# Rotating an 8192 x 8192 matrix: the first loads over four buffers, the last macro tile in two halves with four output buffers

## The chip, the cores and the metric

The kernel runs on one core of a Trainium2 chip. The metric is the device time of one execution in microseconds (us).

PE is the matmul engine, DVE the vector engine, ACT the scalar engine, SP the engine whose queue issues the loads. "DMA engines" are the 16 engines that move data between the memory (HBM) and the core's own memory. One DMA instruction is split over all 16.

## The reference

```python
def reference(x, k):          # x: 8192 x 8192 float32, k = 1
    return np.rot90(x, k)
```

So out[8191 - c, r] = x[r, c]: a transpose with the rows of the result in reverse order. No arithmetic: 268.4 MB are read and 268.4 MB are written.

## The kernel before

The matrix is cut into 16 macro tiles of 1024 rows and 4096 columns. The last of them is cut further, into pieces of 2048, 1024 and 1024 columns. A macro tile has eight loads of 2 MB; each load is reversed in blocks by eight copies on DVE, into 68 small buffers. When all rows of the macro tile are there, PE transposes 4 blocks of 128 columns at a time for all 1024 rows, ACT copies the result out of PE's accumulation memory in two halves, and one store of 2 MB goes out ("an output"). Loads and outputs are numbered 0 to 127 here.

```python
def macro_tiles(N, M):
    for r0 in range(0, N, R):                 # R = 1024
        widths = [W] * (M // W)               # W = 4096
        ...
        if r0 + R == N:
            widths[-1:] = [2048, 1024, 1024]
        ...
    a_pool = ... bufs=2     # load buffers, 2 MB each
    r_pool = ... bufs=68    # reversed chunks, a macro tile needs 64
    o_pool = ... bufs=2     # output buffers, 2 MB each
    for r0, c0, C in tiles:
        last = (r0, c0, C) == tiles[-1]
        q = W // C
        for t0 in range(0, RT, q):
            if loads < 2:
                a = o_pool.tile([P, W], dt, tag="o")
            else:
                a = a_pool.tile([P, W], dt, tag="a")
            loads += 1
            nc.sync.dma_start(out=a, in_=x[...])             # load, issued by SP
            ... 8 x nc.vector.tensor_copy(...[:, :, ::-1])   # reversal on DVE
        for g0 in range(0, C // P, G):                       # G = 4
            ot = o_pool.tile([P, W], dt, tag="o")
            S = PW if last and g0 + G == C // P else G       # PW = 2
            for h in range(0, G, PW):
                ... 16 x nc.tensor.transpose(ps..., chunks..., ident)
                nc.scalar.copy(o[...], ps[:])                # 1.87 us
                done = h + PW
                if done % S == 0:
                    nc.scalar.dma_start(out=dst, in_=o[...]) # store, issued by ACT
```

A load buffer is free again when its eight reversals are done. An output buffer is free when its store has landed.

Of the kernel before, what the change touches and what calls it, by code (L numbers as in the profile page):

```python
# [2 lines left out]

# [5 lines left out]

P = 128  # L10




R = 1024
RT = R // P
W = 4096
CH = 512
G = 4
PW = 2  # L20


def whole_reads(nc):






    for fn in nc.m.functions:  # L30
        for block in fn.blocks:
            for n, ins in enumerate(block.instructions):
                if not isinstance(ins, mybir.InstDMACopy):
                    continue
                src = ins.ins[0]
                ap = [list(d) for d in src.ap]
                if len(ap) == 3 and ap[2][0] == 1 and ap[1][0] == ap[2][1]:
                    ap = [ap[0], [1, 1], [1, ap[1][1] * ap[2][1]]]
                    block.instructions[n] = copy.replace(
                        ins,  # L40
                        ins=[copy.replace(src, ap=ap)],
                        ant_dge_precooked=False,
                    )


def macro_tiles(N, M):

    for r0 in range(0, N, R):
        widths = [W] * (M // W)
        if r0 == 0:  # L50
            widths[:1] = [4096]
        if r0 + R == N:
            widths[-1:] = [2048, 1024, 1024]
        c0 = 0
        for C in widths:
            yield r0, c0, C
            c0 += C


@with_exitstack  # L60
def kernel(
    ctx: ExitStack,
    tc: tile.TileContext,
    x: bass.AP,
    k: bass.AP,
    out: bass.AP,
):
    nc = tc.nc
    assert k == 1, f"only k=1 supported, got {k}"
    nc.at_finalize(whole_reads)  # L70

    N, M = x.shape
    dt = x.dtype

    consts = ctx.enter_context(tc.tile_pool(name="consts", bufs=1))
    ident = consts.tile([P, P], dt)
    make_identity(nc, ident)

    a_pool = ctx.enter_context(tc.tile_pool(name="a_pool", bufs=2))
    r_pool = ctx.enter_context(tc.tile_pool(name="r_pool", bufs=68))  # L80
    o_pool = ctx.enter_context(tc.tile_pool(name="o_pool", bufs=2))
    psum_pool = ctx.enter_context(
        tc.tile_pool(name="psum", bufs=2, space=bass.MemoryType.PSUM)
    )

    tiles = list(macro_tiles(N, M))
    loads = 0
# [3 lines that stand above are left out]
        chunks = {}  # L91
        for t0 in range(0, RT, q):

            if loads < 2:
                a = o_pool.tile([P, W], dt, tag="o")
            else:
                a = a_pool.tile([P, W], dt, tag="a")
            loads += 1
            a = a.rearrange("r (q c) -> r q c", q=q)
            nc.sync.dma_start(  # L100
                out=a,
                in_=x[r0 + t0 * P : r0 + (t0 + q) * P, c0 : c0 + C].rearrange(
                    "(q r) c -> r q c", q=q
                ),
            )


            for u in range(q):
                for j in range(C // CH):
                    ar = r_pool.tile([P, CH // P, P], dt, tag="ar")  # L110
                    nc.vector.tensor_copy(  # L111
                        out=ar[:],
                        in_=a[:, u, j * CH : (j + 1) * CH].rearrange(
                            "r (b m) -> r b m", m=P
                        )[:, :, ::-1],
                    )
                    chunks[t0 + u, j] = ar

        for g0 in range(0, C // P, G):
            ot = o_pool.tile([P, W], dt, tag="o")  # L120
            o = ot.rearrange("m (g f) -> m g f", g=G)
            S = PW if last and g0 + G == C // P else G
            for h in range(0, G, PW):
                ps = psum_pool.tile([P, PW, R], mybir.dt.float32)
                for w in range(PW):
                    g = g0 + h + w
                    for t in range(RT):
                        nc.tensor.transpose(  # L128
                            ps[:, PW - 1 - w, t * P : (t + 1) * P],
                            chunks[t, g * P // CH][:, g % (CH // P), :],  # L130
                            ident,
                        )
                nc.scalar.copy(o[:, G - PW - h : G - h, :], ps[:])  # L133

                done = h + PW
                if done % S == 0:
                    top = M - c0 - (g0 + done) * P
                    dst = out[top : top + S * P, r0 : r0 + R].rearrange(
                        "(g m) f -> m g f", g=S
                    )  # L140
                    nc.scalar.dma_start(  # L141
                        out=dst, in_=o[:, G - done : G - done + S, :]
                    )


# [1 line left out]
_INS = ['x', 'k']  # L147
_OUTS = [((8192, 8192), 'float32')]

_NUMBERS = {'k': 1}  # L150


# [26 lines left out]
```

## Time and profile before

| | before |
|---|---|
| time, median of the first 3 runs | 1275.13 us |
| bytes moved | 537.55 MB |
| rate in the middle | about 428 GB/s |
| bytes at that rate, worked out (537.55 / 0.428) | 1256 us |

The page's first part has the span and the busy time of each engine with its share of the span.

```profile
span 1274.2 us, 10388 instructions
...
PE 719.2 (56%) x4096; PEld 685.5 (54%) x4096; DVE 355.2 (28%) x1024; ACT 466.9 (37%) x257; POOL 0.7 (0%) x6
```

No engine that computes is near its limit. The page's second part cuts the span in 40 slices of 31.9 us; the lines below are the busy share of the DMA engines in tenths, and what they moved.

```profile
DMA  9999999999999999999999999999999999999998
GB/s 375 366 427 427 427 428 431 429 428 428 430 428 430 428 427 429 429 429 429 427 427 427 429 427 428 427 427 429 428 427 426 424 423 429 427 425 422 420 408 338
```

The rate stands at 427 to 431 GB/s in most of the span and is low in the first two slices and the last two. What can be gained without moving fewer bytes lies there.

The timeline shows the start. Each line has start, duration, engine, source line and operation, the number of merged instructions, and in brackets how long the engine stood idle before and what ended that. The lines are the reversals of loads 3 to 7, and the issue of the first store.

```profile
22.76 2.77 DVE L111 COPY ar<-a 128x512 f32<-128x512 f32 x8 [2.12 <-DMA a<-in_x_dram]
...
29.79 2.77 DVE L111 COPY ar<-a 128x512 f32<-128x512 f32 x8 [4.25 <-DMA a<-in_x_dram]
...
35.39 2.77 DVE L111 COPY ar<-a 128x512 f32<-128x512 f32 x8 [2.83 <-DMA a<-in_x_dram]
...
42.46 2.77 DVE L111 COPY ar<-a 128x512 f32<-128x512 f32 x8 [4.29 <-DMA a<-in_x_dram]
...
47.89 2.77 DVE L111 COPY ar<-a 128x512 f32<-128x512 f32 x8 [2.66 <-DMA a<-in_x_dram]
...
54.41 0.64 ACTq L141 DMA_DIRECT2D out_dram<-ot  x1
```

The first four loads come 4.9 us apart, which is full rate for 2 MB. Then the steps are 7.0, 5.6, 7.1 and 5.4 us: only two load buffers are left in rotation, and a load can be issued only when the reversals of the load two before are done.

The end, in windows of 5 us. The columns are the window, its length, the busy time of PE, PE's weight loads, DVE, ACT and POOL with the number of instructions, the granted clock, the busy share of the DMA engines and, last, GB/s.

```profile
1240.00:1245.00 5.00, 3.74 (x32) 3.46 (x32) 0.00 (x0) 2.08 (x2) 0.00 (x0) 1.00 0.91 386
1245.00:1250.00 5.00, 1.76 (x9) 1.76 (x10) 2.77 (x8) 3.64 (x2) 0.00 (x0) 0.83 0.68 288
1250.00:1255.00 5.00, 4.79 (x36) 4.55 (x35) 0.00 (x0) 3.09 (x2) 0.00 (x0) 0.83 0.85 357
1255.00:1260.00 5.00, 3.26 (x30) 2.98 (x29) 0.00 (x0) 3.15 (x3) 0.00 (x0) 1.00 0.90 374
1260.00:1265.00 5.00, 3.05 (x28) 2.77 (x26) 0.00 (x0) 2.49 (x2) 0.00 (x0) 1.00 0.88 374
1265.00:1270.00 5.00, 0.00 (x0) 0.00 (x0) 0.00 (x0) 2.17 (x2) 0.00 (x0) 0.54 0.95 393
1270.00:1275.00 5.00, 0.00 (x0) 0.00 (x0) 0.00 (x0) 0.00 (x0) 0.00 (x0) 0.50 0.45 187
```

From 1245 us on the rate stays at 187 to 393 GB/s: the last outputs share two buffers, each waits for a store to land and then for two copies of ACT.

### The profile page before, as it was taken

How to read it: one execution, taken by the hardware profiler on the slowest of the kernel's cores; microseconds unless marked ns; L12 is line 12 of the kernel's file. 1: busy time of each engine (PE TensorE's matmuls, PEld its weight loads, DVE VectorE, ACT ScalarE, POOL GpSimd, SP SyncE). 2: the span in 40 equal slices, each digit the busy share in tenths (PEclk: the TensorE clock that was granted, in tenths of full speed). 3: DMA queues.
4: the chain of work that ended last, by engine and by line, in shares of the span. 5: the costliest groups of instructions: out<-in, count | busy, mean ns of one | idle time of the engine just before them, and what ended most of it. 6: DMA issues, size and time to landing. Idle time of an engine off the chain costs nothing.

```text
span 1274.2 us, 10388 instructions
## 1 busy us (share of the span) xinstructions
PE 719.2 (56%) x4096; PEld 685.5 (54%) x4096; DVE 355.2 (28%) x1024; ACT 466.9 (37%) x257; POOL 0.7 (0%) x6
## 2 busy tenths in 40 slices
PE   1455556556655665556546565565565665665564
PEld 0355556555554655556546555565555554665564
DVE  4422232223222322232223222322232222321210
ACT  0233343334334333343334333433343333434444
POOL 0000000000000000000000000000000000000000
PEclk9968686877777677776886867768777778678878
DMA  9999999999999999999999999999999999999998
GB/s 375 366 427 427 427 428 431 429 428 428 430 428 430 428 427 429 429 429 429 427 427 427 429 427 428 427 427 429 428 427 426 424 423 429 427 425 422 420 408 338
DMA packets 39105, 537.55 MB, mean 422 GB/s; under 512 B 4112, under 2 KB 4112, under 8 KB 6160
## 3 DMA queue, kind: packets, MB, share of 16 engines
q1 hardware_dynamic: 20480, 268.44, 49.8%
q10 hardware_dynamic: 18576, 268.44, 49.8%
q8 instruction: 32, 0.52, 0.2%
q14 instruction: 17, 0.14, 0.0%
HBM read 268.44 MB, written 268.44 MB: 421 GB/s over the span
## 4 chain that ended last, share of the span: by engine, by line
DMA 84%; DVE 12%; issue 2%; ACT 1%; PE 0%; DVEq 0%; SPq 0%; ACTq 0%
DMA a<-in_x_dram 81%; DVE ar L111 12%; DMA out_dram<-ot 3%; ACT ot L133 1%; PE ps L128 0%; DVEq L111 0%; SPq L100 0%; ACTq L133 0%; ACTq L141 0%
## 5 line engine op out<-in xcount | busy, mean ns | idle before, releaser
L128 PE MATMUL ps<-ident,ar 128*128 128x128 f32 x4096 | 719.2, 358 | 543.8 <-ACT ot L133 500.2
L128 PEld LDWEIGHTS ps<-ident,ar 128*128 128x128 f32 x4096 | 685.5, 192 | 577.3 <-ACT ot L133 530.5
L133 ACT COPY ot<-ps 128x2048 f32<-128x2048 f32 x256 | 465.6, 1870 | 789.3 <-DMA out_dram<-ot 733.5
L111 DVE COPY ar<-a 128x512 f32<-128x512 f32 x1024 | 355.2, 421 | 894.4 <-DMA a<-in_x_dram 894.4
L133 ACT ACT_TABLE_LOAD x1 | 1.3, 1283 | 10.9 <-DVE ar L111 10.9
masks.py:199 POOL TENSOR_SCALAR_AFFINE_SELECT ident<-ident 128x128 f32<-128x128 f32 x1 | 0.3, 292 | 0.1
masks.py:197 POOL MEMSET ident<- 128x128 f32 x1 | 0.2, 204 | 0.3 <-POOLq L160 0.3
L160 POOL MEMSET const-bfloat16-1.0<- 128x1 bf16 x1 | 0.1, 102 | 0.0
L160 POOL MEMSET const-uint8-127<- 128x1 uint8 x1 | 0.1, 102 | 0.0
L160 POOL MEMSET const-float32-0.0<- 128x1 f32 x1 | 0.1, 99 | 0.2 <-issue 0.2
L160 POOL MEMSET const-float32-1.0<- 128x1 f32 x1 | 0.1, 99 | 0.0
## 6 DMA issues: line engine op xcount, KB each, us to landing
a<-in_x_dram SPq DMA_DIRECT2D x128, 2048.0 KB, 16.6
out_dram<-ot ACTq DMA_DIRECT2D x127, 2048.0 KB, 15.9
out_dram<-ot ACTq DMA_DIRECT2D x2, 1024.0 KB, 5.7
```

Of the source, the lines that this page charges most:

```text
L111: nc.vector.tensor_copy(out=ar[:], in_=a[:, u, j * CH : (j + 1) * CH].rearrange("r (b m) -> r b m", m=P)[:, :, ::-1],)
L128: nc.tensor.transpose(ps[:, PW - 1 - w, t * P : (t + 1) * P], chunks[t, g * P // CH][:, g % (CH // P), :], ident,)
L133: nc.scalar.copy(o[:, G - PW - h : G - h, :], ps[:])
L160: nc = _bacc.Bacc("TRN2", target_bir_lowering=False, num_devices=1)
```

## The change

Its intent is to fill both ends. The first eight loads rotate over the two load and the two output buffers (the latter are not needed before the first output), so that loads 4 to 7 need not wait. The last macro tile is cut in two halves of 2048 columns, and the four outputs of the last half alternate between load and output buffers, since no load needs them any more.

```diff
--- before.py
+++ after.py
@@ -14,6 +14,7 @@
 
 R = 1024
 RT = R // P
+LAST = [2048, 2048]
 W = 4096
 CH = 512
 G = 4
@@ -47,10 +48,8 @@
 
     for r0 in range(0, N, R):
         widths = [W] * (M // W)
-        if r0 == 0:
-            widths[:1] = [4096]
         if r0 + R == N:
-            widths[-1:] = [2048, 1024, 1024]
+            widths[-1:] = LAST
         c0 = 0
         for C in widths:
             yield r0, c0, C
@@ -91,7 +90,8 @@
         chunks = {}
         for t0 in range(0, RT, q):
 
-            if loads < 2:
+
+            if loads < RT and loads % 4 >= 2:
                 a = o_pool.tile([P, W], dt, tag="o")
             else:
                 a = a_pool.tile([P, W], dt, tag="a")
@@ -117,7 +117,11 @@
                     chunks[t0 + u, j] = ar
 
         for g0 in range(0, C // P, G):
-            ot = o_pool.tile([P, W], dt, tag="o")
+
+            if last and g0 // G % 2 == 0:
+                ot = a_pool.tile([P, W], dt, tag="a")
+            else:
+                ot = o_pool.tile([P, W], dt, tag="o")
             o = ot.rearrange("m (g f) -> m g f", g=G)
             S = PW if last and g0 + G == C // P else G
             for h in range(0, G, PW):
```

The order of the transposes on PE and of the copies on ACT does not change. The last four loads have half-size (2048 columns) instead of quarter-size rows, so DVE reverses the last 32 chunks in another order.

## The prediction

> **What bounds it.** The DMA. The chain that ended last is 84% DMA; PE is busy 56%, ACT 37%, DVE 28%. The forty slices show 427 to 431 GB/s nearly throughout; only the ends are lower: 375 and 366 in the first two, 408 and 338 in the last two. The Trainium skill ("DMA: Bandwidth & Descriptors", Specifications) gives 435 GB/s as fabric ceiling; the trace's plateau of 428 agrees. 537 MB at 428 GB/s is an estimated 1256 us of the 1274 us span. So some 18 us are lost, at the two ends, part of it unavoidable (first and last latency). The change moves no fewer bytes, so it cannot gain 2% (25 us).
>
> **Start.** The timeline shows reversals starting, as loads land, at 8.1, 13.0, 17.9, 22.8 us (4.9 apart, full rate), then 29.8, 35.4, 42.5, 47.9: loads 4 to 7 rotate over two buffers, and each waits for the reversal (2.77 us) of the load two before. The first load takes 7.4 us from issue to landing, so about 2.5 us of latency lies bare every second load. The last four take 25.1 us instead of 19.6. With four buffers load 7 should land at about 42.4, the first output be issued near 49 instead of 54.4. Windows of 5 us from 0 to 65 lack 8.6 us of transfer against 428 GB/s; 2.3 of it is the first latency, about 0.9 stays. Gain about 5.4 us, all on the critical path: the steady state is bound by bytes and merely shifts.
>
> **End.** Windows of 5 us from 1200 lack about 8.7 us, 2.0 of it the last latency; the worst are 288 GB/s (1245 to 1250), then 357, 374, 374, 393: the last outputs have two buffers, and each waits for a store, then 3.64 us of ACT copies, then the latency. The change gives the last four outputs four buffers, so they run back to back. Against it: all four need the last load. From its landing I count about 7 us to the next output's issue (reversal, transposes, two copies of 1.87 us) plus 2 us to its first bytes, covered only by earlier outputs, still on two buffers. The skill (same page, Queues, rings and completion order) says a DMA engine alternates between rows packet by packet; this fits the trace: with loads of 2048 columns (half-size packets) loads take about 13 us and outputs 7.9, instead of 9.8 each. Replaying the measured durations by hand I estimate the last load landing near 1242 (old clock), two gaps of about 1.5 us, and a gain of about 2.5 us.
>
> **Nothing else moves:** the order of instructions on PE, DVE, ACT is the same; only the last four loads change shape.
>
> **Prediction: 1267 us**, 80% range 1261.5 to 1272. Chances: faster by over 2% 0.01, within 2% 0.98, slower 0.01.
>
> **Right if:** reversals start every 4.9 us through the eighth; the second slice rises from 366 to above 410 GB/s; DVE work is 5 to 6 us earlier from then on; the middle stays at 427 to 431; the last three outputs' ACT copies wait for no store, and the final 20 us run near 428, with one or two short gaps around the last load's landing.
>
> **Wrong if:** the first outputs come too late to fill the time after load 9, giving the start's gain back; or the last load lands after the earlier outputs are gone, opening a gap of 5 us or more before the last four, so the end is even or worse; or the gaps near the end vanish altogether, giving 1262.

## More of the kernel before

The page's third and fourth parts give the DMA queues (packets, MB, share of 16 engines; q1 and q10 carry the kernel's loads and stores) and, last line, the chain of work that ended last, by engine.

```profile
q1 hardware_dynamic: 20480, 268.44, 49.8%
q10 hardware_dynamic: 18576, 268.44, 49.8%
q8 instruction: 32, 0.52, 0.2%
...
DMA 84%; DVE 12%; issue 2%; ACT 1%; PE 0%; DVEq 0%; SPq 0%; ACTq 0%
```

84% of the chain is DMA. The line q8 will matter later: it is not data of the kernel but instructions, 32 packets of 16 KB.

## The result, and the profile after

The changed kernel took 1271.54 us (median of 4 runs, 1271.33 to 1272.35) against 1274.65 us in the same job: ratio 0.9974, 95% interval 0.9951 to 0.9996. A ratio is the mean time of one kernel's fast runs over that of the other's fast runs of the same rounds, so it is not quite the ratio of the medians. Two later jobs gave 0.9963 and 0.9960. So the gain is 3.3 to 5.1 us; the prediction had 8.

The same lines of the page as before, after the change: span, GB/s of the 40 slices, the chain by engine.

```profile
span 1269.5 us, 10387 instructions
...
GB/s 400 416 430 428 429 427 430 430 428 429 428 429 429 428 429 429 428 430 429 429 428 427 423 428 428 429 428 429 425 423 429 428 421 424 424 427 418 421 385 357
...
DMA 79%; ACT 14%; DVE 4%; PE 1%; issue 1%; ACTq 0%; DVEq 0%
```

The second slice rose from 366 to 416 GB/s. The last two, 408 and 338 before, are 385 and 357. The chain is still DMA for the most part, but now 14% of it, some 174 us, is ACT. That is not the end: four outputs are only 15 us of copies. In the middle of the span the chain now runs through outputs (54% of it are stores), with a copy of 3.64 us between one store and the next; before it ran through loads (81%) and their reversals on DVE (12%). The start, same lines of the timeline as before:

```profile
22.69 2.77 DVE L111 COPY ar<-a 128x512 f32<-128x512 f32 x8 [2.12 <-DMA a<-in_x_dram]
...
27.57 2.77 DVE L111 COPY ar<-a 128x512 f32<-128x512 f32 x8 [2.11 <-DMA a<-in_x_dram]
...
32.47 2.77 DVE L111 COPY ar<-a 128x512 f32<-128x512 f32 x8 [2.12 <-DMA a<-in_x_dram]
...
38.17 2.77 DVE L111 COPY ar<-a 128x512 f32<-128x512 f32 x8 [2.93 <-DMA a<-in_x_dram]
...
43.02 2.77 DVE L111 COPY ar<-a 128x512 f32<-128x512 f32 x8 [2.08 <-DMA a<-in_x_dram]
...
49.55 0.65 ACTq L145 DMA_DIRECT2D out_dram<-ot  x1
```

Five steps of 4.9 us, one of 5.7 (32.47 to 38.17), and then 4.9 again; the eighth reversal starts at 43.0 instead of 47.9 us and the first store is issued at 49.6 instead of 54.4. The end, in windows of 5 us, with cuts:

```profile
1195.00:1200.00 5.00, 1.80 (x17) 1.56 (x15) 0.32 (x1) 0.00 (x0) 0.00 (x0) 1.00 0.96 375
...
1205.00:1210.00 5.00, 4.35 (x25) 4.11 (x23) 2.05 (x7) 0.00 (x0) 0.00 (x0) 0.68 1.02 328
...
1230.00:1235.00 5.00, 2.94 (x14) 2.94 (x15) 0.00 (x0) 3.63 (x2) 0.00 (x0) 0.50 0.59 252
...
1240.00:1245.00 5.00, 4.41 (x41) 4.09 (x40) 0.00 (x0) 3.96 (x3) 0.00 (x0) 1.00 0.75 318
1245.00:1250.00 5.00, 4.42 (x41) 4.15 (x40) 0.00 (x0) 4.00 (x3) 0.00 (x0) 1.00 0.99 419
...
1255.00:1260.00 5.00, 0.29 (x3) 0.05 (x1) 0.00 (x0) 2.58 (x2) 0.00 (x0) 0.94 1.00 419
...
1265.00:1270.00 5.00, 0.00 (x0) 0.00 (x0) 0.00 (x0) 0.00 (x0) 0.00 (x0) 0.50 0.28 115
```

The low stretch from 1245 on is gone. In its place there are two windows with a gap (252 and 318 GB/s), two slow windows earlier (375 and 328), and the final drain stays at 413 to 419, with 115 in the last window. I counted what the windows lack of 428 GB/s, until the end of the span: 8.7 us from 1200 us on before, 9.0 us from 1195 us on after. **The loss at the end moved; it did not shrink.**

The waits of ACT in the last 30 us, before (first) and after (second): who it waited for, total us, times, longest.

```profile
ACT ot L133 <- DMA out_dram<-ot: 8.6, 3, 4.2
ACT ot L133 <- PE ps L128: 1.9, 1, 1.9
```

```profile
ACT ot L137 <- PE ps L132: 2.7, 4, 0.7
```

The waits for a store are gone, as intended. So what the change was made to remove was removed, and the time did not follow. That is what the experiments are about.

### The profile page after: what moved, and what is told of

It reads as the page before. It is cut to its first block, busy times and chain, and to the rows that moved or that the text cites. A ratio compares the mean times of both kernels' runs of the same rounds, so it can differ in the third digit from the quotient of the medians.

```text
span 1269.5 us, 10387 instructions
## 1 busy us (share of the span) xinstructions
PE 705.9 (56%) x4096; PEld 665.4 (52%) x4096; DVE 355.2 (28%) x1024; ACT 467.5 (37%) x257; POOL 0.7 (0%) x6
## 4 chain that ended last, share of the span: by engine, by line
DMA 79%; ACT 14%; DVE 4%; PE 1%; issue 1%; ACTq 0%; DVEq 0%
DMA out_dram<-ot 54%; DMA a<-in_x_dram 25%; ACT ot L137 14%; DVE ar L111 4%; PE ps L132 1%; ACTq L145 0%; ACTq L137 0%; DVEq L111 0%
## 5 line engine op out<-in xcount | busy, mean ns | idle before, releaser
L132 PE MATMUL ps<-ident,ar 128*128 128x128 f32 x4096 | 705.9, 352 | 549.4 <-ACT ot L137 469.4
L132 PEld LDWEIGHTS ps<-ident,ar 128*128 128x128 f32 x4096 | 665.4, 188 | 589.6 <-ACT ot L137 501.0
```

The source lines that it names most:

```text
L132: nc.tensor.transpose(ps[:, PW - 1 - w, t * P : (t + 1) * P], chunks[t, g * P // CH][:, g % (CH // P), :], ident,)
```

## The experiments

Where an experiment compares two kernels of one job, both were measured beside the kernel before, in the same five rounds on the same chip. An edit is shown against the changed kernel unless said otherwise.

### 1. The two parts by themselves

My theory was that the start delivers its gain and the end gives nothing.

**Start alone** (the end as before):

```diff
-LAST = [2048, 2048]
+LAST = [2048, 1024, 1024]
-            if last and g0 // G % 2 == 0:
+            if False:
```

> Only the first loads rotate over four buffers; the last macro tile is split 2048, 1024, 1024 as before. My theory (the start delivers, the end does not): the first eight loads land 4.9 us apart, the transferred bytes run 5.5 to 6 us ahead of the kernel before from 50 us on, and nearly all of it arrives at the end: 1268.5 to 1270 us, ratio about 0.9955. Rival (the start's gain is given back later, in the middle or at the old end): ratio 0.9975 to 1.0.

Measured: 1272.0 us against 1276.6 us, ratio 0.9969 (0.9957 to 0.9982), so 4.0 us (0.0031 x 1276). The loads do land 4.9 us apart and the transferred bytes are 5.9 us of transfer ahead of the kernel before at 100 us and 6.4 us ahead at 1140 us. But of these 6 us only 4 reach the end, by the ratio's interval between 2.3 and 5.5. That is between the two expectations, and it does not exclude the 5.4 us of the prediction.

**End alone** (the start as before):

```diff
-            if loads < RT and loads % 4 >= 2:
+            if loads < 2:
```

> Only the last macro tile is changed (two halves of 2048, the last four outputs over four buffers); the first loads as before. My theory: even or worse than before by up to 2 us (ratio 1.000 to 1.0015), with gaps of about 2 and 1.3 us in the DMA some 35 us before the end, where the outputs of the first half wait for one of two buffers. Rival (the end gains the 2.5 us predicted, the start is what fell short): ratio 0.998.

Measured: 1276.27 us, ratio 1.0006 (0.9993 to 1.0019). The end gains nothing; the predicted 2.5 us (0.998) is outside the interval.

**End alone, but all outputs on two buffers:**

```diff
-            if loads < RT and loads % 4 >= 2:
+            if loads < 2:
-            if last and g0 // G % 2 == 0:
+            if False:
```

> The last macro tile in two halves of 2048, but all outputs on two buffers; the first loads as before. If the four buffers do useful work in the changed kernel, this is slower than the run with them alone by 3 to 5 us (six outputs instead of two wait about 1 to 2 us each for a store, copies and the DMA's latency): ratio 1.002 to 1.004. If the buffers do not matter, equal to it.

Measured: 1276.29 us, ratio 1.0005 (0.9992 to 1.0017). A miss: the four buffers were to be worth 3 to 5 us over two, and are worth nothing that can be measured (by the means 0.2 us, the other way round, with two standard errors of 1.1). Experiment 4 looks for the reason.

**The whole change again:**

> The changed kernel itself, timed in five rounds beside its parts. Expected 1271 to 1272 us, ratio 0.9970 to 0.9978 as in the first result; if the parts add up, its difference from before is the sum of that of the start alone and of the end alone, within 1 us.

Measured: 1271.08 us, ratio 0.9963 (0.9951 to 0.9976), a little below the ratio expected. The parts add up: 4.0 us from the start, nothing from the end, 4.7 us for both, within the intervals.

These rounds hold a second reading of each part. "End alone" and the whole change differ only in the start: 1276.54 against 1271.10 us by the means, so 5.4 us (give or take 0.8; this and the like below are two standard errors, from the scatter of the runs). "Start alone" and the whole change differ only in the end: 1271.86 against 1271.10, so 0.8 us (give or take 0.7). In full length the start is thus worth 4.0 to 5.4 us, the end somewhere between nothing and 1 us.

### 2. Where does the start's gain go on the way?

A load or store counts as landed when the slowest of its 16 DMA engines is done. The trace has the 16 landings of every DMA. From them, the time between the first and the last engine of a DMA (median over the stretch):

```
stretch of the span      before     start alone
100 to 200 us            3.6 us     2.5 us
1000 to 1130 us          4.6 us     8.3 us
```

And the lead of the start alone over the kernel before, in one profile of each, at the same number of reversals and of issued stores:

```
number    reversal   store issue   mean
16        4.2 us     8.2 us        6.2 us
110       2.7 us     7.3 us        5.0 us
119       2.7 us     5.0 us        3.9 us
```

In this pair the bytes stay 6 us ahead, the finished DMAs do not. My reading: in the long middle the engines drift apart, the fast ones run ahead as far as the buffers let them, and the lead of the whole bytes is partly theirs. It is worth nothing at the end, since the slowest engine decides.

The other full-length profiles bear this out only in part. From 1000 to 1130 us the two others with the old start ("end alone" and the same on two buffers) have 5.7 and 6.6 us between first and last engine, the eight with the changed start 7.6 to 8.4. The lead of the changed kernel at the last landing of a load, from load 16 to load 110, falls from 6.0 to 4.1 us over "end alone", but over the run on two buffers it goes from 5.3 to 6.1 and does not fall. So how much of the lead is lost differs from profile to profile.

If the reading is right, the gain must depend on how long the middle is. The rival is that the old end meets the loads and stores in another phase and gives back the same amount whatever the length. I ran both kernels over the first and the last 1024 rows only, 4 macro tiles instead of 16 (the result is wrong: the other rows of x are not turned):

```diff
-    for r0 in range(0, N, R):
+    for r0 in (0, N - R):
```

> The kernel before, but only the first and the last 1024 rows of x are turned (4 macro tiles instead of 16; the result is wrong on purpose): the length over which the 16 DMA engines can drift apart is a quarter. Serves as the base of start_short. About 1275 minus three quarters of 1252 us (12 macro tiles of 78.2 us each at the pace of the middle), so 335 to 340 us.

> The start change alone, in the same shortened form (wrong on purpose). In the full length the start alone gained 4.0 us, though 5.8 us of bytes were ahead. My theory: the difference is lost because in the long middle the engines drift further apart (first to last engine of one DMA 8 us instead of 4.6), and with a quarter of the length they drift less: start_short is 5 to 6 us faster than before_short, and the spread of its landings before the end is under 4 us. Rival (what is given back is due to the form of the end, met in another phase, whatever the length): 4 us faster or less, as in full length.

Measured: 332.59 (335 to 340 were expected) and 324.89 us, so 7.7 us faster by the medians, with landings about 2.5 us apart in the middle of the short run with the changed start. A second job with the same two kernels:

> The kernel before, shortened, again as base of these rounds: 331 to 334 us; start_short_2 is 6 to 8 us faster than it, where the start alone gained 4 us in full length.

> The start change alone, shortened, again as base of these rounds: 324.5 to 325.5 us.

Measured: 333.19 and 325.76 us, 7.4 us. With the new end in both kernels (the two runs of experiment 3) it is 332.47 against 324.69 by the means, 7.8 us. So the start's gain is 7.4 to 7.8 us over a quarter of the length and 4.0 to 5.4 us over the whole. The rival has fallen as I had put it: the end is the same in both lengths, and does not give back the same amount. That the gain is smaller over the long middle is shown; that the drift of the engines makes it so is argued, since no run changes the drift alone. The gain in the short form is more than the 5 to 6 us I had expected and more than the lead of bytes (5.8 us); I have no full account of the excess. One part points the right way: in the short kernel before, the engines are 3.7 to 4.6 us apart, in the one with the changed start 2.5.

### 3. Is the new end worth more while the engines are close together?

The theory was that the end's 2.5 us are eaten by the same spread. Then they must show in the short form. The edits are those of experiment 2 on the changed kernel and on the end alone.

> The whole change in the shortened form (4 macro tiles, wrong on purpose). Compared with start_short_2 of the same rounds it shows what the new end is worth where the engines are little apart (spread of landings about 2.5 us instead of 8). Theory (the end's gain of 2.5 us is eaten by the engines being apart when the last tile begins): 1.5 to 3 us faster than start_short_2. Rival (the new end is worth nothing by its own form, whatever the spread): within 1 us of start_short_2.

> The end change alone in the shortened form (wrong on purpose), against before_short_2 of the same rounds. Theory: faster by 1 to 3 us. Rival: within 1 us of it, as in full length.

Measured: the whole change 324.75 us against 325.76 for the start alone; the end alone 332.93 us against 333.19. By the means, 0.9 us (give or take 0.8) and 0.5 us (give or take 1.6). The second pair decides little, but the first excludes the 2.5 us. The theory has fallen: the new end measures under 1 us by its own form, with the engines together or apart.

### 4. Why four buffers do not beat two at the end

This needs no new run. The ACT timeline of the last five outputs of "end alone" (four buffers): the issues of its stores.

```profile
1246.06 0.55 ACTq L145 DMA_DIRECT2D out_dram<-ot  x1
...
1250.38 0.55 ACTq L145 DMA_DIRECT2D out_dram<-ot  x1
...
1254.69 0.55 ACTq L145 DMA_DIRECT2D out_dram<-ot  x1
...
1259.00 0.55 ACTq L145 DMA_DIRECT2D out_dram<-ot  x1
...
1261.55 2.31 ACTq L145 DMA_DIRECT2D out_dram<-ot  x2
```

And of "halves on two buffers": the issue of the same first store, two copies that wait for a store, and the last issue.

```profile
1247.43 0.55 ACTq L145 DMA_DIRECT2D out_dram<-ot  x1
1248.61 3.63 ACT L137 COPY ot<-ps 128x2048 f32<-128x2048 f32 x2 [1.22 <-DMA out_dram<-ot]
...
1254.22 3.63 ACT L137 COPY ot<-ps 128x2048 f32<-128x2048 f32 x2 [1.97 <-DMA out_dram<-ot]
...
1267.85 2.31 ACTq L145 DMA_DIRECT2D out_dram<-ot  x2
```

With four buffers the last issue comes 15.5 us after the first (1261.55 - 1246.06), with two 20.4 us (1267.85 - 1247.43). Now the landings of these five stores, for the first, the 15th and the 16th DMA engine to land (us, from the records of the trace; for output 127 its second half):

```
              four buffers                two buffers
output 123    1252.6  1252.7  1252.8      1254.0  1254.1  1254.1
output 124    1257.5  1257.7  1259.8      1258.9  1259.0  1259.8
output 125    1262.4  1262.7  1264.5      1264.4  1264.5  1265.9
output 126    1267.4  1267.6  1269.4      1270.0  1270.2  1270.8
output 127    1272.3  1272.6  1274.3      1275.0  1275.2  1275.7
```

Fifteen engines finish 26.5 us after the first issue with four buffers and 27.8 with two: they gain 1.2 us, where 3 to 5 were expected. But one engine falls 2 us behind at output 124 and stays behind, because it never stands idle again. With two buffers it falls behind as well, by 0.8 and then 1.4 us, and catches up to 0.5 while the others wait for the next store. The 16th engine ends 28.2 us after the first issue with four buffers and 28.3 with two. **By these landings, the gaps that four buffers closed had been the slow engine's time to catch up.** The three profiles of the changed kernel repeat it: 26.5 to 26.6 us for 15 engines, 28.1 to 28.3 for the 16th.

The kernel before needs 31.2 us from the issue of output 123 to the last landing (1242.11 to 1273.3), so the halves do shorten the last five outputs by 3 us. But in "end alone" output 123 is issued 4 us later, at 1246.06: what the drain gains, the outputs before it have lost.

What holds up that one engine? In the trace of "end alone" a packet of q8, the PE's instructions, 16 KB in 0.97 us, starts at 1257.8 us; with two buffers at 1259.2. In all eleven full-length profiles an engine falls behind in the store that lands around the last such packet, or in the next one. It is so at the start too: the step of 5.7 us after the change (32.47 to 38.17) is load 6, of which 15 engines land by 37.4 us and one at 38.1, with an instruction packet of 8 KB (of another queue, q14) at 36.7. Until load 9 one engine stays 0.8 us behind, load after load. That the packet causes it is an inference from this coincidence; the delay of about 2 us is also twice the packet's own 0.97 us, and I cannot say why. A quarter more of these packets was the next experiment.

### 5. More instructions to fetch

Every fourth transpose is done twice (the result stays right). PE is far from its limit, so by itself this should cost nothing.

```diff
-                    for t in range(RT):
+                    for t in [0, 0] + list(range(1, RT // 2)) + [RT // 2] + list(range(RT // 2, RT)):
                         nc.tensor.transpose(
```

> The changed kernel once more, as the base for the two other runs of these rounds: ratio 0.9960 to 0.9975.

> The changed kernel with every fourth transpose done twice (5120 instead of 4096 on an engine that is busy 56%; the result stays right). The PE's instructions come by DMA in packets of 16 KB, one per about 39 us, each some 1.0 us on one DMA engine; they go from 32 to 40. Theory A (these fetches load one or few DMA engines more than the others, and so push the engines apart and make the last engine late): slower than the changed kernel by 2 to 5 us (8 packets of 0.6 us each if alone on the slowest engine), with a wider spread of landings in the middle. Theory B (the drift has another source, or the fetches are spread evenly): within 0.6 us of the changed kernel, spread as before, about 8 us.

Busy time and the instruction queue in the page of this run:

```profile
PE 759.8 (60%) x5120; PEld 722.6 (57%) x5120; DVE 355.0 (28%) x1024; ACT 467.5 (37%) x257; POOL 0.7 (0%) x6
...
q8 instruction: 40, 0.66, 0.2%
```

PE has 60% instead of 56%, and the packets of q8 are 40 instead of 32, as planned; that they grow with the transposes (5120 instead of 4096) shows whose instructions they are. Measured: 1273.74 us (1273.06 to 1274.0) against 1271.7 (1271.09 to 1272.41) for the changed kernel in the same rounds (ratios 0.9974 and 0.9960), so 1.8 us more by the means. 0.13 MB more to move would be 0.3 us at 428 GB/s. The effect is just under theory A's 2 to 5 us and well over B's 0.6; but the spread of landings, which A wanted wider, is 8.3 us in both. So the run lost more than the bytes of its fetches; if the fetches are the cause, each cost about 0.2 us. The loss builds up in the middle, not in the tail: output 110 already lands 2.0 us later than in the changed kernel of the same rounds (mean of the 16 engines). Whether it comes through single engines stays open: the trace does not tell which engine a packet used, and PE's own extra work was not separated from the fetches.

### 6. Other ends

**The last macro tile whole**, so that the tail has loads of full rows and eight outputs over four buffers:

```diff
-LAST = [2048, 2048]
+LAST = [4096]
```

> The changed kernel with the last macro tile in one piece of 4096 columns (loads in 16 KB rows as everywhere), its eight outputs alternating over four buffers. After the last load all eight outputs are left. If splitting the last tile is what costs (loads starved by half-size packets, outputs on two buffers while loads wait, a store waiting for a load's landing), this has one gap of about 3 to 4 us after the last load instead of several and is 0 to 3 us faster than the changed kernel: ratio 0.994 to 0.9965. If splitting hides more than that, it is slower than the changed kernel by 2 to 5 us: ratio 0.998 to 1.0.

Measured: 1270.0 us, ratio 0.9954 (0.9941 to 0.9966).

**Stores of 1 MB** for all outputs of both halves:

```diff
-            S = PW if last and g0 + G == C // P else G
+            S = PW if r0 + R == N and C < W else G
```

> The changed kernel, but all outputs of the two halves are stored in two pieces of 1 MB, each as soon as its 1.87 us copy is done. If the two gaps near the end (about 2.0 and 1.3 us) are there because an output on two buffers waits for a store and then for both copies, each shrinks by up to 1.9 us: 1 to 3 us faster than the changed kernel, ratio 0.994 to 0.9955. If the end is bound by something else (spread of the engines, the loads), equal to the changed kernel within 0.6 us.

Measured: 1270.82 us, ratio 0.9956 (0.9943 to 0.9968). Both are 0.5 to 1.1 us below the changed kernel by the ratios (of its two later jobs), which is inside the intervals, so neither is shown to be better by itself. The page of the whole last tile has two gaps (windows in us):

```profile
1212.00:1217.00 5.00, 1.75 (x7) 1.35 (x7) 0.00 (x0) 3.63 (x2) 0.00 (x0) 0.70 0.42 180
...
1221.00:1226.00 5.00, 4.79 (x42) 4.32 (x40) 0.00 (x0) 3.89 (x3) 0.00 (x0) 1.00 0.41 174
```

They lack 2.9 and 3.0 us ((428 - 180) x 5 / 428, and the same with 174). The first waits for the output ahead of the last load's landing, the second for the first one after it. So I took both ideas:

**Whole last tile, its outputs and the one ahead of them in stores of 1 MB:**

```diff
+LAST = [4096]
+            S = PW if last or (r0 + R == N and c0 + 2 * W == M and g0 + G == C // P) else G
```

> The last macro tile in one piece, its eight outputs over four buffers, and those outputs and the one ahead of them stored in two pieces of 1 MB. The whole last tile alone left gaps of about 2.7 us at the last load's landing and 2.7 us after the first store behind it. If these gaps are the wait for both copies, each shrinks by up to 1.9 us: 2 to 3.5 us faster than the whole last tile, ratio 0.9925 to 0.994. If the spread of the engines fills the gap instead: ratio 0.995, no better.

Measured: 1269.92 us (1268.48 to 1270.51), ratio 0.9942 (0.9929 to 0.9956), against 1271.7 us (1271.09 to 1272.41) for the changed kernel in the same rounds. It beats both kernels: 7.2 us under the one before and 2.2 us under the changed one, by the means. Against the whole last tile alone (0.9954, in another job) the intervals overlap, and 0.9942 lies between the two expectations, so that the stores of 1 MB add anything is not shown. Its windows:

```profile
1212.00:1217.00 5.00, 1.76 (x7) 1.36 (x7) 0.00 (x0) 3.50 (x2) 0.00 (x0) 0.55 0.88 364
...
1221.00:1226.00 5.00, 4.79 (x36) 4.55 (x35) 0.00 (x0) 3.46 (x2) 0.00 (x0) 0.82 0.32 134
```

The first gap shrank to 0.7 us, the second did not (3.4 us): there the second copy of the output waits for PE until 1223.55 us, and the first half's store is issued no earlier than that, though its copy began at 1220.72.

## Why the prediction was right or wrong

**"The DMA bounds the kernel; the change cannot gain 2%": right.** The middle of the span is unchanged, and all gains measured are below 0.6%.

**"Start: gain about 5.4 us, all on the critical path ... the steady state merely shifts": right in size at the start, not safe after it.** At 100 us the lead of bytes is 5.8 us. In full length 4.0 us of it reach the end by one comparison and 5.4 by the other, so the size is not refuted. But the steady state does not merely shift: over a quarter of the length the same start is worth 7.4 to 7.8 us. Bytes ahead are not time ahead; that the drift of the engines makes the difference is my reading of it. A smaller miss: load 7 was to land at 42.4 us and did at 43.0, because load 6 had one late engine.

**"The change gives the last four outputs four buffers, so they run back to back ... gain about 2.5 us": this is the step that failed.** The outputs do run back to back, but the gain is about nil: the end alone has ratio 1.0006 (0.9993 to 1.0019, which excludes 2.5 us), and beside the new start it is worth 0.8 us. The cost it had wrong is that of the drain and of the outputs before it. The two gaps that I expected, 1.5 us each, are there: 2.1 and 1.3 us, worked out from the windows with 252 and 318 GB/s. What I left out are two other terms. First, in a drain without waits the late engine does not catch up, so the last store lands on one engine 1.7 us after the 15 others, where it was 0.6 us in the kernel before; the last window lacks 3.2 us, where I took 2.0 over from the kernel before. Second, the slow windows at 1195 and 1205 us, 1.8 us together, which I took to go away with the rest. That these terms are there is read from the windows and landings; what makes one engine late stays open.

**"All four need the last load; from its landing I count about 7 us to the next output's issue": this did not bind.** The timeline after the change, around the last load:

```profile
1236.49 2.77 DVE L111 COPY ar<-a 128x512 f32<-128x512 f32 x8 [10.86 <-DMA a<-in_x_dram]
1236.68 3.64 ACT L137 COPY ot<-ps 128x2048 f32<-128x2048 f32 x2 [2.90 <-DMA out_dram<-ot]
...
1240.35 0.55 ACTq L145 DMA_DIRECT2D out_dram<-ot  x1
1241.01 1.87 ACT L137 COPY ot<-ps 128x2048 f32<-128x2048 f32 x1 [0.69 <-PE ps L132]
```

The last load has landed at 1236.49. The copy of the next output, 124, begins at 1241.01 and waits less than a microsecond; it stands behind the copies of output 123, which waited for a store until 1236.68. So the gaps come from the outputs of the first half on their two buffers, not from the last load.

**"The last three outputs' ACT copies wait for no store": right**, by the waits shown above. **"The final 20 us run near 428": nearly**, 413 to 419.

**The total.** 7.9 us were forecast as 5.4 + 2.5; measured are 4.0 to 5.4 and about 0 to 0.8 for the parts, and 3.3 to 5.1 for the whole. The measured 1271.54 us lies in the stated range, near its upper edge, but that owes more to the width of the range than to the account: the gain is about half of what was forecast.

What the document calls from the Trainium skill: the round-robin by packets between queue rows ("DMA: Bandwidth & Descriptors", Queues, rings and completion order) agrees with this trace, where (timeline before, reversals and store issues) loads of half-size packets come about 13 us apart and outputs 7.9, instead of 9.8 each, when the last tile is being loaded. "Packet" is here the trace's record of 8 or 16 KB; that the page means the same by it is not shown. The same page (Why a DMA increments its semaphore by 16 and not by 1) says that the 16 engines of one DMA finish independently; here that is 0.4 us apart in the first loads and 8 us after a millisecond.

## What to carry to other kernels

In a kernel bound by DMA, bytes ahead are not time ahead: look at the landing of the slowest of the 16 engines, and allow for a lead won early to shrink over a long middle (here 7.4 to 7.8 us over a quarter of the length, 4.0 to 5.4 over all of it). Before closing small gaps near the end, ask what uses them; here, by the landings, one engine used them to catch up, and back-to-back stores ended no earlier. For this tail, smaller pieces of the first stores, together with a last tile of full rows, took another 2.2 us off the changed kernel; which of the two did it was not separated.

## What the Trainium skill lacked or had wrong

- "Runtime: NRT & Kernel Launch", Instruction fetch mechanics, calls the cost of crossing a 16 KiB boundary "one DMA tail-bump, mostly hidden". In this DMA-bound kernel 32 such packets move (q8, about 1 us each), and at the end of eleven profiles one of the 16 engines falls up to 2 us behind in the store that lands around such a packet or next; 8 packets more, with 1024 transposes more, went with 1.8 us more. That the packets are the cause is not shown.
- "DMA: Bandwidth & Descriptors", Specifications, lists about 358 GB/s as the limit of HBM per core. This core, with reads and writes together, holds 427 to 431 GB/s. "HBM Reference", Specifications, says that a core alone measures about 425.
- No page that I read says that the 16 engines drift apart over a long stream: first to last landing of a DMA 1.9 to 2.8 us early and 7.6 to 8.4 us after a millisecond in the eight full-length profiles with the changed start, 3.0 to 4.2 and 4.6 to 6.6 us in the three with the old one.
